# A transformer layer's feed-forward in two phases, all up products first, and the down-projection by seven products of sums

## The chip, the cores and the metric

The kernel runs on one core of a Trainium2 chip. The core has a matrix engine (TensorE, PE in the profile), three engines for elementwise work (VectorE, DVE; ScalarE, ACT; GpSimd, POOL) and a queue engine (SyncE, SP) that issues most transfers between the chip's large memory (DRAM) and the on-chip memory (SBUF). Products are accumulated in PSUM, in banks of 128 x 512 float32. Each engine works through its own instructions in order; engines wait for each other by semaphores. The metric is the device time of one execution in microseconds (us).

## The reference

One layer over 2048 rows of 1024: a retention branch and an attention branch, an output projection, and a feed-forward with a squared ReLU. The change touches the feed-forward, the last lines here:

```python
def _sqrelu_mlp(h, w1, w2):
    return jnp.square(jax.nn.relu(h @ w1)) @ w2
...
    x = x + g1 * (jnp.concatenate([ret, att], axis=-1) @ w_out)
    h2 = _modulate(_rmsnorm(x, norm2_g), sh2, sc2)
    x = x + g2 * _sqrelu_mlp(h2, w_ff1, w_ff2)
...
    return _rmsnorm(x, final_norm_g)
```

`w_ff1` is 1024 x 4096 and `w_ff2` 4096 x 1024. `g2` is one row of 1024 factors, the gate.

## The kernel before

Every float32 factor of a product is written as a sum of two float16 parts, a high one and a low one. The high part is a rounding copy on ScalarE (L70), the low part a subtraction on VectorE or GpSimd (L71). A product is then three TensorE products: high x high, high x low, low x high.

The 2048 rows are 16 tiles of 128, in two halves of 8 (`halves`). The hidden width is 16 blocks of 256 (`FB`, `NB`), and the loop over `b` runs 32 times: all blocks for the first half, then all for the second. One pass has two parts:

- The up part (`up_part`, L1522 to L1524) multiplies a block of `w_ff1` with the half's activations. It treats both as 2 x 2 block matrices and forms the result from seven products of sums instead of eight products (Winograd's form of Strassen's method). The sums of the activations are made once per half (`h_pair`, by GpSimd and ScalarE) and kept as seven 1 MB tiles `hf`; those of the first half go through DRAM. The sums of w1 are made for each pass by GpSimd (`sum_w1`, L1451) and split by ScalarE and VectorE (`form_w1`, L1460 and L1461). Each of the seven products is 12 matmuls into one bank. `up_out` adds the banks up on VectorE (L1545), applies the ReLU on ScalarE (L1533), squares on GpSimd (L1534) and splits the result into `uhi` and `ulo`.
- The down part (`down`, L1582 to L1584) multiplies the block's 256 hidden columns with 256 rows of `w_ff2`, tile by tile and 512 columns at a time, in the plain way: 16 times 6 matmuls. VectorE adds each bank into one of eight accumulators (L1585). Before that GpSimd multiplies the block of `w_ff2` with the gate (L1506), and ScalarE and VectorE split it (L70, L71 on `ws`).

So one pass has 7 x 12 = 84 up matmuls and 96 down matmuls of 128 x 128 by 128 x 512.

The accumulators start as the tiles' residual rows `x1_d` and stay in SBUF for a half. When the first half ends, each is normalised and stored (`ending`, L1600) and loaded anew for the second half. The second half's activation sums are made during the first half (`pairs`), and the first pass's up products are partly issued during attention (`prelude`). Work that is due at no fixed place, such as the last tile's transposes (L1306) or the endings, goes through the list `rest`, of which a few steps are issued after each product. In this stage the order of instructions on every engine is that in which the Python code issues them; only the stage of input projections at the kernel's start is ordered by a scheduler.

## Time and profile before

| | us |
|---|---|
| median of 3 runs | 2948.83 |
| lowest, highest run | 2946.54, 2952.58 |
| span of the profiled execution | 2938.2 |
| TensorE busy within the span | 2770.0 |
| first up matmul, last down matmul start | 1644.4, 2927.3 |

The span is counted from the first to the last instruction of the profiled execution, the only time that the page gives for it; the runs' times hold some work around it as well. In the profile a row of a group gives the line of the code, engine, operation, the tiles written and read, their shapes and the count; then the busy time in us and the mean of one instruction in ns; then the engine's idle time just before these instructions, and what ended it. A row of a timeline gives start and duration in us, and in brackets the idle time before. A row of windows gives a stretch, its length, and for each engine the busy time in it and the number of instructions.

### The profile page before, as it was taken

Reading aid. Unit: us, or ns where it says so; the run is one execution under the profiler, and the core shown is the slowest. Engines: PE = TensorE matmul, PEld = TensorE weight load, DVE = VectorE, ACT = ScalarE, POOL = GpSimd, SP = SyncE. Lnnn points to the kernel's source line nnn. Section 1 sums busy time; section 2 is a strip of 40 time slices with the busy share of each in tenths; the row PEclk is TensorE's granted clock in tenths of the full one; section 3 lists DMA queues with packets and bytes.
Section 4 is the critical chain, followed back from the end, with each engine's and each line's share of the span. In section 5 each row is a group of like instructions: output and inputs, shape, how many; then the busy total and the mean of one; then the engine's idle time right before and its main releaser. Section 6 shows DMA issues by size and latency. Waiting matters only on the chain. (4 is left out here: it accounts for less than half of the span.)

```text
span 2938.2 us, 45295 instructions
## 1 busy us (share of the span) xinstructions
PE 2770.0 (94%) x17140; PEld 1644.8 (56%) x17140; DVE 2181.9 (74%) x3330; ACT 1389.6 (47%) x2279; POOL 1546.1 (53%) x1275
## 2 busy tenths in 40 slices
PE   7998898998889999999999899999999999999998
PEld 3787677775556666555666444444444344444443
DVE  5889847647887777777876577778777777777776
ACT  2333333325777777787777433333332333333323
POOL 2436426425776668787656656664443444444332
PEclk9999999999999999999999999999999999999999
DMA  8988843526412123332211723331114411111111
GB/s 299 336 291 284 275 154 102 159 69 203 135 43 84 50 63 121 89 102 89 72 64 51 276 90 101 104 105 58 53 51 154 169 64 48 51 51 54 58 44 58
DMA packets 265161, 346.95 MB, mean 118 GB/s; under 512 B 106215, under 2 KB 163815, under 8 KB 263150
## 3 DMA queue, kind: packets, MB, share of 16 engines
q1 hardware_dynamic: 254662, 336.57, 34.6%
q10 hardware_dynamic: 10280, 7.48, 0.9%
q8 instruction: 135, 2.21, 0.3%
q14 instruction: 84, 0.69, 0.1%
HBM read 272.52 MB, written 71.46 MB: 117 GB/s over the span
## 5 line engine op out<-in xcount | busy, mean ns | idle before, releaser
L178 DVE TENSOR_REDUCE nm<-mp 128x1 f32<-128x512 f32 (+1 forms) x576 | 391.1, 685 | 169.0 <-PE mp L165 140.8
L219 POOL TENSOR_TENSOR plo<-p,phi 128x1024 f16<-128x1024 f32 x160 | 352.7, 2205 | 173.4 <-ACT phi L212 131.7
L208 ACT ACTIVATE p<-st 128x512 f32<-128x512 f32 x576 | 338.5, 597 | 188.4 <-PE st L203 116.7
L1582 PE MATMUL pd<-w2hi,uhi 128*128 128x512 f16 x1024 | 388.0, 379 | 11.7 <-DVE acc L1585 10.8
L1583 PE MATMUL pd<-w2lo,uhi 128*128 128x512 f16 x1024 | 388.0, 379 | 0.8 <-DVE w2lo L71 0.8
L1584 PE MATMUL pd<-w2hi,ulo 128*128 128x512 f16 x1024 | 388.1, 379 | 0.0
L1585 DVE SCALAR_TENSOR_TENSOR acc<-pd,sc,acc 128x512 f32<-128x512 f32 x512 | 366.5, 739 | 5.6 <-PE pd L1584 5.6
L1522 PE MATMUL pu<-hf,w1f 128*128 128x512 f16 x896 | 340.3, 380 | 2.4 <-DVE q L1545 2.0
L1524 PE MATMUL pu<-hf,w1f 128*128 128x512 f16 x896 | 340.3, 380 | 0.0
L1523 PE MATMUL pu<-hf,w1f 128*128 128x512 f16 x896 | 340.1, 380 | 0.0
L824 PE MATMUL pso<-whi,hi_l 128*128 128x512 f32 (+1 forms) x768 | 294.1, 386 | 11.5 <-ACT xs L524 6.7
L212 ACT ACTIVATE phi<-p 128x1024 f16<-128x1024 f32 x288 | 304.0, 1055 | 0.0
L826 PE MATMUL pso<-whi,lo_l 128*128 128x512 f32 (+1 forms) x768 | 292.1, 381 | 4.2 <-DVE lo_l L67 4.2
L825 PE MATMUL pso<-wlo,hi_l 128*128 128x512 f32 (+1 forms) x768 | 291.6, 380 | 1.2 <-DVE wlo L67 1.1
L235 PE MATMUL o<-wv,plo 128*128 128x65 f16 x2304 | 235.2, 193 | 25.4 <-POOL plo L219 16.7
L221 DVE TENSOR_TENSOR plo<-p,phi 128x512 f16<-128x512 f32 x256 | 242.7, 949 | 18.9 <-ACT phi L212 16.0
L236 PE MATMUL o<-wv,phi 128*128 128x129 f16 x2304 | 243.0, 220 | 0.0
L235 PEld LDWEIGHTS <-plo 128*128 128x128 f16 x2304 | 206.2, 98 | 59.9 <-POOL plo L219 25.7
L202 PE MATMUL st<-qr,ks 128*128 128x512 f16 x576 | 219.3, 381 | 15.4 <-ACT p L208 15.3
L1534 POOL TENSOR_TENSOR r<-r 128x512 f32<-128x512 f32 x64 | 66.4, 1041 | 294.9 <-ACT r L1533 294.9
L203 PE MATMUL st<-qr,ks 128*128 128x512 f16 x576 | 219.3, 381 | 0.1
L236 PEld LDWEIGHTS <-phi 128*128 128x128 f16 x2304 | 205.4, 97 | 19.9 <-issue 0.3
(324 smaller groups left out, 5734.8 us busy)
## 6 DMA issues: line engine op xcount, KB each, us to landing
wm<-in_w_ff SPq DMA_DIRECT2D x64, 512.0 KB, 5.5
w1r<-in_w_ff SPq DMA_DIRECT2D x64, 512.0 KB, 4.5
ws<-in_w_ff SPq DMA_DIRECT2D x124, 256.0 KB, 3.3
wst<-in_w_in SPq DMA_DIRECT2D x60, 512.0 KB, 5.2
wst<-in_w_mod SPq DMA_DIRECT2D x32, 512.0 KB, 6.0
hf<-hp SPq DMA_DIRECT2D x56, 256.0 KB, 3.1
hf<-hf SPq DMA_DIRECT2D x14, 1024.0 KB, 6.2
orv<-rv SPq DMA_DIRECT2D x35, 256.0 KB, 4.0
```

Source lines behind the costliest of these rows:

```text
L178: nc.vector.tensor_reduce(dst, src, axis=AX.X, op=ALU.max, negate=True)
L208: nc.scalar.activation(self.p[kt // 2][:, kt % 2], self.s.pop(kt), AF.Exp, scale=HD**-0.5)
L219: nc.gpsimd.tensor_tensor(lo, p, hi, op=ALU.subtract)
L235: mm(o[:, : HD + 1], lo[:, i, c], v[:, : HD + 1], start=False, stop=False)
L236: mm(o, hi[:, i, c], v[:, :VW], start=False, stop=last)
L1522: mm(pu[i], whi, hi, start=k == 0, stop=False)
L1523: mm(pu[i], whi, lo, start=False, stop=False)
L1524: mm(pu[i], wlo, hi, start=False, stop=k == 3)
L1582: mm(ps, uh, wh, start=f == 0, stop=False)
L1583: mm(ps, uh, wl, start=False, stop=False)
L1584: mm(ps, ul, wh, start=False, stop=f == NF - 1)
L1585: nc.vector.scalar_tensor_tensor(acc[:, c], ps, sc2, acc[:, c], op0=ALU.mult, op1=ALU.add)
```

## The change

The feed-forward is taken apart into two phases.

Phase one (`up_jobs`) makes all up products. Its passes are called items: blocks 0 to 5 for the first half alone, then blocks 6 to 15 for both halves with one set of w1 forms, then blocks 0 to 5 for the second half alone. While the first items run, the second half's activation sums are made, now straight into SBUF (`form` for half 1, its low parts by turns on GpSimd and VectorE). The squared results are not split but stored to DRAM as float32 (`store_u`). Beside the products `w2_steps` makes the seven forms of each block of `w_ff2` once, split, without the gate, and stores them to DRAM (`wf_d`).

Phase two (`down_jobs`) makes the down-projection. The 16 blocks form four rounds of four (`PLACE`). In each round the seven forms of four blocks stand in SBUF, seven tiles of 1 MB, in the slots that held the activation sums. A round goes through eight pairs of tiles (`PAIRS`). For a pair, four pieces of u are loaded two pairs ahead; GpSimd makes their four sums and ScalarE and VectorE split seven forms one pair ahead (`prepare`); TensorE makes seven products of 12 matmuls (`down`); VectorE adds them up (`down_out`); GpSimd multiplies each of the four 128 x 512 results with the gate and adds it to the tile's rows (`gate`), which are loaded from `x1_d` and stored there again in rounds 0 to 2 (`write`). In round 3 they are normalised and go to the output (`ending`). PSUM has six banks for both phases. The gate and the scale factors are folded together differently in `scales`.

The diff, cut to its core:

```diff
-    hf_d = [scratch(f"hf{i}", 7, [P, 2, 4, 512], F16) for i in range(2)]
+    hf_d = scratch("hf", 7, [P, 2, 4, 512], F16)
+    u_d = [scratch(f"u{i}", 2, [4, P, 4, 4, P]) for i in range(4)]
+    wf_d = [scratch(f"wf{i}", 7, [P, 4, 2, 512], F16) for i in range(4)]
...
         def form(i, w):
+            if hf == 1:
+                f = hs[1, i][:, :, :, j * P : (j + 1) * P]
+                split16(f[:, 0], f[:, 1], x[w], nc.gpsimd if i % 2 else nc.vector)
+                return
...
+    AHEAD = 6
+    ITEMS = [(b, (0,)) for b in range(AHEAD)] + [(b, (0, 1)) for b in range(AHEAD, NB)]
+    ITEMS += [(b, (1,)) for b in range(AHEAD)]
+    PLACE = {b % NB: ((b - AHEAD) // 4, (b - AHEAD) % 4) for b in range(AHEAD, AHEAD + NB)}
...
+        ff["w"] = Ring((pool(early_ff, "fw"), "w", 7))
+        ff["r"] = Ring((pool(early_ff, "fr"), "r", 6))
+        ff["ps"] = Ring((pool(early_ff, "fp1", space=PSUM), "p", 4))
...
+        ff["w"].extend(pool(late_ff, "fw2", side="right"), "w", 3)
+        ff["r"].extend(pool(late_ff, "fr2", side="right"), "r", 5)
+        ff["ps"].extend(pool(late_ff, "fp2", space=PSUM), "p", 2)
...
-    def down(b, m, n, acc):
...
-        nc.vector.scalar_tensor_tensor(acc[:, c], ps, sc2, acc[:, c], op0=ALU.mult, op1=ALU.add)
...
+    def store_u():
+        _, b, hf, blk, r = stores.pop(0)
+        rd, slot = PLACE[b]
+        dst = u_d[rd][hf][:, :, blk, slot].rearrange("q p t -> p q t")
+        nc.sync.dma_start(dst, r.rearrange("p (q t) -> p q t", q=4))
...
+    def w2_steps(b):
+        x = {}
+        rd, slot = PLACE[b]
+        def fetch(f):
+            w = xp.tile([P, D], F32, name="w2r", tag="hb", bufs=2)
+            nc.sync.dma_start(w, a["w_ff2"][0, b * FB + f * P : b * FB + (f + 1) * P, :])
+            x[f"b{f + 1}1"], x[f"b{f + 1}2"] = w[:, :512], w[:, 512:]
+        def add(to, p, q, at=None):
+            x[to] = x[at] if at else xp.tile([P, 512], F32, name="w2s", tag="hu", bufs=3)
+            nc.gpsimd.tensor_tensor(x[to], x[p], x[q], op=ALU.subtract)
+        def form(i, w):
+            f = xp.tile([P, 2, 512], F16, name="w2f", tag="hp", bufs=2)
+            nc.scalar.activation(f[:, 0], x[w], AF.Copy, scale=scw)
+            nc.vector.scalar_tensor_tensor(f[:, 1], x[w], scw, f[:, 0], op0=ALU.mult, op1=ALU.subtract)
+            x["made"] = i, f
+        def store():
+            if "made" in x:
+                i, f = x.pop("made")
+                nc.sync.dma_start(wf_d[rd][i][:, slot], f)
+        steps = [(add, "t1", "b12", "b11"), (form, 0, "b11"), (add, "t2", "b22", "t1")]
+        steps += [(form, 5, "t1"), (add, "t3", "b22", "b12", "b12"), (form, 2, "t2"), (add, "t4", "b21", "t2", "t1")]
+        steps += [(form, 1, "b21"), (form, 3, "t3"), (form, 6, "b22"), (form, 4, "t4")]
+        def step(fn, *at):
+            store()
+            fn(*at)
+        return [lambda f=f: fetch(f) for f in range(2)] + [lambda at=at: step(*at) for at in steps] + [store]
...
+    def up_jobs():
+        pairs = [step for j in range(4) for step in h_pair(1, j)]
+        later = [step for b in PLACE for step in w2_steps(b)]
+        owed = 0.0
+        for n, (b, halves_) in enumerate(ITEMS):
+            both = len(halves_) == 2
+            if 1 in halves_:
+                rest_steps(len(rest))
+                while pairs:
+                    pairs.pop(0)()
+            last0 = max(m for m, (_, h) in enumerate(ITEMS) if 0 in h)
+            for i in range(4 if n == 0 else 0, 7):
+                for hf in halves_:
+                    for k in range(4):
+                        up_part(n, i, hf, k)
+                    ff["job"] += 1
+                    while stores and stores[0][0] < ff["job"] - 1:
+                        store_u()
+                    if hf == halves_[-1]:
+                        if n > 0 and i < 4:
+                            sum_w1(n + 1, *SUMS1[i])
+                        if n > 0 or i > 3:
+                            form_w1(n + 1, i)
+                        if i == 4:
+                            fetch_w1(n + 2)
+                    up_out(n, i, hf)
+                    if rest:
+                        rest_steps(2)
+                    elif pairs:
+                        pairs.pop(0)()
+                        if pairs and i % 2:
+                            pairs.pop(0)()
+                    elif later and n > AHEAD - 1:
+                        owed += 1.5
+                        while later and owed >= 1:
+                            owed -= 1
+                            later.pop(0)()
+                    if n == last0 + 1:
+                        fetch_w2(0, i)
+                    if n == len(ITEMS) - 1:
+                        prepare(0, i - 1)
+            if n == len(ITEMS) - 2:
+                assert not later, len(later)
+                for blk in RAW:
+                    fetch_u(0, blk)
+                fetch_y(0)
+        while later:
+            later.pop(0)()
+        while stores:
+            store_u()
+        prepare(0, 6)
...
+    def fetch_w2(rd, i):
+        w = w2[rd, i] = ff["h"][rd % 2].tile([P, 4, 2, 512], F16, name="w2", tag="hf")
+        nc.sync.dma_start(w, wf_d[rd][i])
+    def fetch_u(p, blk):
+        if p < len(PAIRS):
+            rd, hf, q = PAIRS[p]
+            if "raw" not in rings:
+                rings["raw"] = Ring((xp, "w1s", 4), (xp, "hu", 3))
+                rings["sum"] = Ring((xp, "hp", 2), (xp, "u", 2))
+                rings["y"] = Ring((xp, "xr", 3), (xp, "hb", 2))
+            w = raw2[p, NAMES[blk]] = rings["raw"].tile([P, 4, P], F32, "ur")
+            nc.sync.dma_start(w, u_d[rd][hf][q, :, blk])
+    def fetch_y(p):
+        if p < len(PAIRS):
+            for g, t in enumerate(tiles_of(p)):
+                y = ys[p, g] = rings["y"].tile([P, D], F32, "y")
+                nc.sync.dma_start(y, x1_d[t])
+    def sum_u(p, to, x, y, op, at=None):
+        s = raw2[p, to] = raw2[p, at] if at else rings["sum"].tile([P, 4, P], F32, "us")
+        nc.gpsimd.tensor_tensor(s, raw2[p, x], raw2[p, y], op=op)
+    def prepare(p, i):
+        if p >= len(PAIRS) or i < 0:
+            return
+        if i == 0:
+            sum_u(p, "s1", "a21", "a22", ALU.add)
+            sum_u(p, "s2", "s1", "a11", ALU.subtract)
+        if i == 1:
+            sum_u(p, "s3", "a11", "a21", ALU.subtract, "a21")
+        if i == 3:
+            sum_u(p, "s4", "a12", "s2", ALU.subtract, "s2")
+        u = uf[p, i] = ff["w"].tile([P, 2, 4, P], F16, "uf")
+        split16(u[:, 0], u[:, 1], raw2[p, FORMS2[i]])
+    def down(p, i):
+        rd = PAIRS[p][0]
+        ps = pu[i] = ff["ps"].tile([P, 512], F32, "pd")
+        u, w = uf.pop((p, i)), w2[rd, i]
+        for b in range(4):
+            mm(ps, u[:, 0, b], w[:, b, 0], start=b == 0, stop=False)
+            mm(ps, u[:, 0, b], w[:, b, 1], start=False, stop=False)
+            mm(ps, u[:, 1, b], w[:, b, 0], start=False, stop=b == 3)
+    def down_out(p, i):
+        ps = pu.pop(i)
+        def add(x, to=None):
+            to = to if to is not None else ff["r"].tile([P, 512], F32, "d")
+            nc.vector.tensor_tensor(to, ps, xs_[x], op=ALU.add)
+            return to
+        if i == 0:
+            xs_["x"] = ff["r"].tile([P, 512], F32, "d")
+            nc.scalar.activation(xs_["x"], ps, AF.Copy)
+        elif i == 1:
+            gates.append((p, 0, 0, add("x")))
+        elif i == 2:
+            xs_["u2"] = add("x")
+        elif i == 3:
+            xs_["u3"] = add("u2")
+        elif i == 4:
+            gates.append((p, 1, 0, add("u3")))
+        elif i == 5:
+            gates.append((p, 1, 1, add("u3", xs_["u3"])))
+            add("u2", xs_["u2"])
+        elif i == 6:
+            gates.append((p, 0, 1, add("u2", xs_["u2"])))
+    def gate(fast=False):
+        p, g, n, c = gates.pop(0)
+        s = slice(n * 512, (n + 1) * 512)
+        y = ys[p, g][:, s]
+        eng = nc.vector if fast else nc.gpsimd
+        eng.tensor_tensor(c, c, ff["g2"][:, s], op=ALU.mult)
+        eng.tensor_tensor(y, y, c, op=ALU.add)
+        if PAIRS[p][0] < 3:
+            if (g, n) in ((1, 1), (0, 1)):
+                written.append((p, g))
+            return
+        if n == 0:
+            sums[p, g] = ff["sm"].tile([P, 2], F32, name="ss", tag=f"ss{g}")
+        junk = ff["sm"].tile([P, 512], BF16, name="junk", tag="junk", bufs=1)
+        nc.scalar.activation(junk, y, AF.Square, accum_out=sums[p, g][:, n : n + 1])
+        if n == 1:
+            ending(p, g)
+    def write():
+        p, g = written.pop(0)
+        nc.sync.dma_start(x1_d[tiles_of(p)[g]], ys.pop((p, g)))
+    def ending(p, g):
+        ss, y, t = sums.pop((p, g)), ys.pop((p, g)), tiles_of(p)[g]
+        rest.append((lambda: nc.vector.tensor_tensor(ss[:, :1], ss[:, :1], ss[:, 1:], op=ALU.add),))
+        steps = []
+        r = rsqrt_chain(ss[:, :1], 1, 1.0 / D, "e", steps)
+        rest.extend((step,) for step in steps)
+        def whole(c):
+            nc.vector.scalar_tensor_tensor(y[:, c], y[:, c], r, ff["fg"][:, c], op0=ALU.mult, op1=ALU.mult)
+        def store(c):
+            nc.sync.dma_start(out[0, t * P : (t + 1) * P, c], y[:, c])
+        if p == len(PAIRS) - 1:
+            for i in range(2):
+                c = slice(i * 512, (i + 1) * 512)
+                rest.extend([(whole, c), (store, c)])
+        else:
+            c = slice(0, D)
+            rest.extend([(whole, c), (lambda: None,), (store, c)])
+    def down_jobs():
+        for i in range(7):
+            fetch_w2(1, i)
+        for blk in RAW:
+            fetch_u(1, blk)
+        for p, (rd, hf, q) in enumerate(PAIRS):
+            final = p == len(PAIRS) - 1
+            for i in range(7):
+                down(p, i)
+                prepare(p + 1, i)
+                if i in (2, 3, 4, 5):
+                    fetch_u(p + 2, RAW[i - 2])
+                rest_steps(3)
+                if i == 5:
+                    fetch_y(p + 1)
+                while gates and not final:
+                    gate()
+                down_out(p, i)
+                if final:
+                    while gates:
+                        gate(i > 4)
+                if written and i in (1, 2):
+                    write()
+                if (hf, q) == (1, 3) and rd in (0, 1):
+                    fetch_w2(rd + 2, i)
+        while gates:
+            gate(True)
+        rest_steps(len(rest))
```

328 lines of the change are left out of this document (92 added, 236 removed).

## The prediction

> **What bounds the kernel now.** I read the page first: its head, then the chain that ended last.
>
> ```profile
> span 2938.2 us, 45295 instructions
> PE 2770.0 (94%) x17140; PEld 1644.8 (56%) x17140; DVE 2181.9 (74%) x3330; ACT 1389.6 (47%) x2279; POOL 1546.1 (53%) x1275
> PE 32%; DVE 2%; ACT 1%; issue 1%; POOL 0%; DMA 0%; SPq 0%; DVEq 0%; POOLq 0%; ACTq 0%
> ```
>
> TensorE fills the span and the chain, whose six largest lines are the feed-forward's products. Shares over the span say nothing of one stage, so next the windows view (us; busy time and count on PE, PEld, DVE, ACT, POOL; granted clock; DMA share; GB/s).
>
> ```profile
> 1630.00:1650.00 20.00, 19.16 (x134) 10.40 (x132) 11.94 (x22) 10.35 (x21) 11.83 (x13) 1.00 1.03 414
> 1680.00:1705.00 25.00, 20.07 (x90) 8.66 (x89) 23.01 (x29) 8.57 (x15) 15.40 (x12) 1.00 0.83 307
> 1770.00:1790.00 20.00, 18.96 (x88) 8.45 (x87) 15.63 (x21) 6.82 (x11) 13.90 (x10) 1.00 0.68 197
> 2280.00:2335.00 55.00, 47.85 (x210) 20.77 (x209) 44.90 (x54) 21.87 (x37) 23.77 (x21) 0.97 0.48 168
> 2306.00:2312.00 6.00, 4.94 (x16) 1.90 (x16) 5.07 (x7) 1.96 (x3) 2.22 (x2) 0.72 0.55 199
> 2340.00:2900.00 560.00, 560.00 (x2596) 253.79 (x2594) 412.50 (x546) 181.44 (x288) 226.09 (x172) 1.00 0.16 51
> 2598.99:2637.84 38.85, 38.85 (x182) 17.64 (x181) 28.87 (x39) 12.61 (x20) 15.82 (x14) 1.00 0.17 54
> ```
>
> From 2340 to 2900 TensorE never rests, while VectorE has a quarter free and GpSimd more than half. The last row is one block of 256 hidden columns, from one start of its GpSimd sums to the next: 84 up and 96 down products in 38.85 us, 0.2158 us each. (The window touches 182 of them at its edges.) TensorE rests only in the first block (4.9 us), at 1780 (1.0) and at the turn between the halves (7.2).
>
> The page says nothing of what GpSimd and VectorE do to each other; the timelines of the two engines at the block's start do.
>
> ```profile
> 2597.30 1.73 POOL L1506 TENSOR_TENSOR ws<-ws,g2b 128x512 f32<-128x512 f32 x1
> 2598.99 1.27 POOL L1451 TENSOR_TENSOR w1s<-w1r 128x512 f32<-128x512 f32 x1
> 2600.34 1.60 POOL L1451 TENSOR_TENSOR w1s<-w1s,w1r 128x512 f32<-128x512 f32 x1
> 2637.84 1.27 POOL L1451 TENSOR_TENSOR w1s<-w1r 128x512 f32<-128x512 f32 x1
> ...
> 2599.14 1.67 DVE L1461 SCALAR_TENSOR_TENSOR w1f<-w1r,sc,w1f 128x512 f16<-128x512 f32 x1
> 2600.74 0.74 DVE L1585 SCALAR_TENSOR_TENSOR acc<-pd,sc,acc 128x512 f32<-128x512 f32 x1
> 2603.73 0.68 DVE L71 TENSOR_TENSOR w2lo<-ws,w2hi 128x512 f16<-128x512 f32 x1
> 2604.99 0.74 DVE L1461 SCALAR_TENSOR_TENSOR w1f<-w1s,sc,w1f 128x512 f16<-128x512 f32 x1
> ```
>
> L1461 takes 0.74 us alone and 1.67 us when it starts beside the sum at 2598.99; it ends 0.55 us behind it. The next sum starts meanwhile and takes 1.60 us instead of 1.27. L1585, which reads PSUM, takes 0.74 us beside a busy GpSimd. So GpSimd and a VectorE instruction with two SBUF inputs take turns, and a turn costs GpSimd up to 1.73 - 1.27 = 0.46 us; PSUM readers cost it nothing.
>
> **A, products removed.** The up-projection keeps its 2688. The down-projection goes from 3072 to 32 pairs of tiles x 7 x 12 = 2688. 384 x 0.2158 = **-82.9 us**, if TensorE stays the bound.
>
> **B, stalls that lose their cause.** No down product follows the first block and no accumulators are swapped at the turn: -4.9 - 1.0 - 7.2 = **-13.1**. Against that, the last tile's transposes move one product (12 matmuls) ahead, to a place where TensorE already waits:
>
> ```profile
> 1678.56 0.66 PE L1306 MATMUL bank<-ident,xr 128*128 128x128 f32 x4 [3.88 <-POOL xr L1301]
> ```
>
> 12 x 0.2158 = **+2.6**; between 0 and 2.6, as the store that L1301 waits for meets fewer loads.
>
> **C, hand-over between the phases.** SP issues, in this order: the last stores of u, the seven 1 MB forms of w2 for round 1 (they wait for TensorE's last use of the slots), then u for pair 1. ScalarE's split of that u stands ahead of its copy of pair 0's first product, so with six PSUM banks TensorE stops after six products, 6 x 2.59 = 15.5 us.
>
> ```profile
> L1545 DVE TENSOR_TENSOR q<-pu,q 128x512 f32<-128x512 f32 x64 | 43.3, 677 | 0.0
> L1533 ACT ACTIVATE r<-r,scu 128x512 f32<-128x512 f32 x64 | 45.8, 722 | 152.2 <-DVE r L1545 152.1
> L1534 POOL TENSOR_TENSOR r<-r 128x512 f32<-128x512 f32 x64 | 66.4, 1041 | 294.9 <-ACT r L1533 294.9
> L70 ACT ACTIVATE uhi<-r 128x512 f16<-128x512 f32 x64 | 39.4, 616 | 3.7 <-POOL r L1534 3.7
> L1550 ACT ACTIVATE v<-pu 128x512 f32<-128x512 f32 x32 | 18.5, 577 | 12.3 <-PE pu L1524 12.3
> hf<-hf SPq DMA_DIRECT2D x14, 1024.0 KB, 6.2
> hb<-h SPq DMA_DIRECT2D x16, 512.0 KB, 5.7
> ```
>
> The last store can go one addition, one relu and one square after the last up product: 0.7 + 0.7 + 1.0 = 2.4 us. Then 7.34 MB at the 414 GB/s of the first window take 17.7 us, and three pieces of u (0.79 MB) 1.9. One 1 MB load lands after 6.2 us where its bytes would need 2.5, so 3.7 of latency are added. Split and copy take 1.2. Pair 0's first bank is free at 2.4 + 17.7 + 1.9 + 3.7 + 1.2 = 26.9, and TensorE has stood 26.9 - 15.5 = 11.4. A stopped TensorE also loses clock: in the row 2306:2312 the grant is 0.72, that is 3.4 of 6.0 us at half rate, 1.7 us lost. Together **+13.1**; between 4 (if the u of pair 1 gets past the loads in front of it by more than half their time) and 20 (if the seven loads run at 300 GB/s, as around 1680 to 1705).
>
> [...]
>
> **D, GpSimd in phase two.** A pair gives TensorE 84 x 0.2158 = 18.13 us. GpSimd gets 12 operations of two SBUF inputs: four sums of u, and gate and addition for four pieces. (Before, the gate went onto w2.) Free, they take 12 x 1.27 = 15.2. VectorE makes seven low parts per pair, each with two SBUF inputs, and a GpSimd that hardly pauses meets all of them: 15.2 + 7 x 0.46 = **18.4**, just above TensorE's 18.13. VectorE's other seven instructions read PSUM and take no turn. VectorE itself has 7 x about 1.2 (between the 0.68 and 1.67 above) + 7 x 0.68 = 13.2, ScalarE 7 x 0.62 + 0.58 = 4.9; both stay below TensorE. Round 3 adds two roots and two whole-row scalings:
>
> ```profile
> L1506 POOL TENSOR_TENSOR ws<-ws,g2b 128x512 f32<-128x512 f32 x120 | 187.5, 1584 | 13.6 <-DMA ws<-in_w_ff 13.6
> L1009 POOL TENSOR_SCALAR cv_e<-ss 128x2 f32<-128x2 f32 x6 | 1.2, 194 | 30.8 <-ACT junk L1594 30.8
> L1010 POOL TENSOR_TENSOR cy_e<-cv_e,half 128x1 f32<-128x1 f32 x1 | 0.5, 549 | 0.1
> 2929.86 1.29 DVE L1600 SCALAR_TENSOR_TENSOR acc<-acc,cy_e,fgb 128x1024 f32<-128x1024 f32 x1 [1.02 <-POOL cy_e L1010]
> ```
>
> The roots take 2 x (0.19 + 0.55) = 1.5. L71's 0.68 us hold GpSimd for 0.46, so 0.22 of an instruction hold nothing; L1600's 1.29 then hold 1.07, two of them 2.1. Round 3 asks 18.4 + 3.6 = 22.0 per pair. GpSimd's lag grows by 0.27 x 24 pairs = 6.5, then by 3.9 x 7 = 27; the last pair, without sums or low parts, wins back some 5. Six banks and u's lead of a pair let TensorE run ahead for a while, but what lag is not worked off is paid at the end: **+28**. At a mean price x for the twelve operations the term is 31 x (12x - 18.13) + 7 x 3.6 - 5 = 372x - 542. Its ends are 0 (at 1.27 round 3 needs 18.8 at most, which the banks cover) and 102 (every operation at 1.73). L1506's mean of 1.584 would give 47; I take 18.4 / 12 = 1.53, because there are only seven turns for twelve operations. A root also waits for ScalarE's square and VectorE's sum of it, with the next gates behind it: up to 1 us each, taken as 0 where the next pair's sums stand in between, 7 to 14 if not.
>
> **E, first items of phase one.** In items 1 to 5 (one half, 18.13 us) GpSimd has four squares at L1534's 1.04 (4.2), four sums of w1 (5.1), ten of the thirteen steps of a second-half tile pair (10/13 of four sums and three low parts, 6.9) and some ten turns (4.5):
>
> ```profile
> L71 POOL TENSOR_TENSOR hp<-hb,hp 128x512 f16<-128x512 f32 x32 | 42.4, 1327 | 19.2 <-ACT hp L70 14.0 <-issue 5.2
> ```
>
> That is 20.7 us, a lag of 13 over five items, and each pair's loads (5.7 us for hb) hold up the sums behind them. Forms are made a whole item ahead and six banks hide about 13 us; items 6 to 15 (36.3 us, some 29 of GpSimd's and 30 of VectorE's work, w2's forms included) win it back. **+4**; between 0 and 22 (four loads not hidden). Without those roomy items w2's forms would cost their GpSimd time.
>
> **F, the rest.** At the end gate and addition stand behind the last product on VectorE, 2 x 0.68 = **+1.4**. Phase two moves 3.1 MB per pair, 174 GB/s; round changes add 7.3 MB and 7 us of backlog, hidden by u's two pairs of lead. The scheduler reorders a few projections: 0, plus or minus 3.
>
> **Sum.** -82.9 - 13.1 + 2.6 + 13.1 + 28 + 4 + 1.4 = -46.9: the span of 2938.2 becomes 2891.3. The runs' median of 2948.83 lies 10.6 above the profiled span; with that kept, the time is **2902**.
>
> **Rivals.** (1) GpSimd never binds: turns fall into its pauses, D = 0, **2874**. For it: 226 of 560 us busy before. Against: 15.2 of 18.13 leave few pauses. (2) The first items starve: E at 22, **2920**; six banks speak against it. (3) Slower: in phase two every GpSimd operation pays a turn, at 1.73 as in the row at 2597.30; D = 102, **2976**. Terms other than D leave 74.9 us of gain, so the point is 372x - 542 = 75, an average of 1.66 us per operation: only 0.13 above what I take. For it: L1506's mean is already 1.584. Against: seven turns in twelve operations.
>
> **Chances.** Forecast 0.47 (alone 2882 to 2925), rival 1 0.20, rival 2 0.13, rival 3 0.15, others 0.05. The range 2866 to 2950 holds the first three and leaves out rival 3 and some tails. 0.2% (6 us) is what a measurement here can tell: faster 0.78, same 0.05, slower 0.17.
>
> **What would show it.** A: 5376 feed-forward products, 0.216 us apart. C: one TensorE gap of about 12 us at the first down products, ended by ScalarE, behind a load of u. D: GpSimd some 18 us busy per pair, its group means near 1.5; TensorE gapless in rounds 0 to 2 and waiting in round 3. E: no gap before item 6. Wrong if gaps appear in rounds 0 to 2, if the gate and addition average over 1.66, or if round 3 runs at 18.1 us per pair.

## The result, and the profile after

The changed kernel takes 3031.53 us in the median of 4 runs (3028.91 to 3033.76); the kernel before, run beside it, 2947.68 us (2945.55 to 2952.58). The ratio is 1.0284, with a 95% interval of 1.0269 to 1.0299: 84 us slower. The forecast was 2902 us, with a range of 2866 to 2950.

The page of the changed kernel, its head and the chain that ended last:

```profile
span 3027.1 us, 45947 instructions
PE 2731.4 (90%) x16756; PEld 1614.5 (53%) x16756; DVE 2045.8 (68%) x3086; ACT 1409.7 (47%) x2349; POOL 1933.3 (64%) x1549
POOL 1%; issue 0%; DVE 0%; ACT 0%; POOLq 0%; DVEq 0%
```

TensorE has less work than before (2731.4 us against 2770.0), and the span has grown by 88.9. No engine is full on average, and the shares of the chain do not say where TensorE stood still. The windows do, when they are cut at the first products of the stages (columns as in the prediction; the last two cuts lie within 0.5 us of theirs). First the kernel before, from a gap that both traces show in the last tile of attention: the first item's 84 up products and what stands among them, then the rest.

```profile
1639.19:1681.65 42.46, 36.69 (x177) 17.29 (x177) 19.82 (x29) 16.39 (x32) 23.75 (x23) 1.00 0.81 301
1681.65:2938.20 1256.55, 1231.17 (x5681) 556.02 (x5679) 936.67 (x1216) 426.02 (x685) 565.88 (x433) 1.00 0.24 79
```

Then the changed kernel: from the same gap to item 1; items 1 and 2; items 3 to 5; items 6 to 16; item 17; pair 0 of phase two; pairs 1 to 24 (rounds 0 to 2); pairs 25 to 30 (round 3).

```profile
1639.32:1694.10 54.78, 42.89 (x181) 19.95 (x181) 20.49 (x28) 15.89 (x31) 18.73 (x18) 0.84 0.52 192
1694.10:1730.36 36.26, 36.26 (x171) 16.43 (x169) 19.16 (x23) 16.03 (x27) 29.82 (x23) 1.00 0.43 138
1730.36:1806.13 75.77, 59.84 (x254) 25.59 (x253) 44.01 (x52) 29.56 (x49) 46.14 (x36) 0.93 0.41 125
1806.13:2249.30 443.17, 398.80 (x1764) 174.41 (x1764) 280.82 (x333) 191.29 (x294) 260.00 (x195) 0.97 0.55 174
2249.30:2282.00 32.70, 20.21 (x85) 8.53 (x85) 18.76 (x21) 13.15 (x21) 19.06 (x14) 0.89 0.94 353
2358.16:2400.09 41.93, 20.77 (x85) 8.83 (x84) 14.00 (x17) 9.64 (x17) 12.56 (x10) 0.73 0.70 260
2400.09:2835.22 435.13, 435.13 (x2015) 197.19 (x2014) 280.90 (x336) 107.48 (x189) 425.73 (x289) 1.00 0.62 207
2835.22:2988.20 152.98, 123.89 (x508) 52.31 (x507) 80.74 (x107) 42.05 (x96) 103.87 (x95) 0.91 0.38 118
```

The way to read them is to set a stage's length beside 0.2158 us for each of its products. Items 1 and 2 (168 products, 36.25 us) and pairs 1 to 24 (18.13 us each) run at TensorE's own pace. Items 6 to 16 have 1764 products, 380.7 us, and take 443.17. No other engine is busy for even two thirds of that stretch. The clock is part of it: the mean grant of 0.97 is worth some 13 us of the 443.17. (The products' busy time, 398.80 us, is 18 above 380.7; the part that the clock does not explain is, as an estimate, the end of the matmul before each rest, since a matmul shows 0.386 us in the group view below but starts 0.2158 us behind the one before.) So a stretch in which everyone has time loses 62 us; the group view of items 6 to 16 shows who waits for whom.

```profile
L1503 PE MATMUL pu<-hf,w1f 128*128 128x512 f16 x588 | 226.8, 386 | 43.1 <-DVE r L1515 37.7 <-ACT hf L70 4.7
L1515 DVE TENSOR_TENSOR r<-pu,r 128x512 f32<-128x512 f32 x147 | 97.3, 679 | 0.0
L1519 ACT ACTIVATE r<-r,scu 128x512 f32<-128x512 f32 x84 | 60.1, 721 | 151.5 <-DVE r L1515 151.5
L1520 POOL TENSOR_TENSOR r<-r 128x512 f32<-128x512 f32 x84 | 91.4, 1091 | 151.4 <-ACT r L1519 146.8 <-DMA wf<-w2f 2.6 <-DMA w1r<-in_w_ff 2.0
```

TensorE waits for VectorE's additions to free a bank. The additions themselves wait for nothing that this view names (0.0), and ScalarE's relu stands idle 1.8 us before each of 84 for them. The timelines of the two engines at the turn from item 11 to item 12 show what is late (start, duration, instruction, in brackets the idle time before it):

```profile
2056.63 0.68 DVE L1515 TENSOR_TENSOR r<-pu,r 128x512 f32<-128x512 f32 x1
2058.71 0.75 DVE L1564 SCALAR_TENSOR_TENSOR w2f<-w2s,scw,w2f 128x512 f16<-128x512 f32 x1 [1.40 <-ACT w2f L1563]
2059.38 1.53 DVE L1488 SCALAR_TENSOR_TENSOR w1f<-w1r,sc,w1f 128x512 f16<-128x512 f32 x1
2060.83 0.68 DVE L1515 TENSOR_TENSOR r<-pu,r 128x512 f32<-128x512 f32 x1
2062.90 1.02 DVE L1564 SCALAR_TENSOR_TENSOR w2f<-w2s,scw,w2f 128x512 f16<-128x512 f32 x1 [1.40 <-ACT w2f L1563]
2063.85 1.28 DVE L1515 TENSOR_TENSOR r<-pu,r 128x512 f32<-128x512 f32 x2
...
2057.34 0.72 ACT L1519 ACTIVATE r<-r,scu 128x512 f32<-128x512 f32 x1 [1.57 <-DVE r L1515]
2057.97 0.71 ACT L1563 ACTIVATE w2f<-w2s,scw 128x512 f16<-128x512 f32 x1
2061.54 0.72 ACT L1519 ACTIVATE r<-r,scu 128x512 f32<-128x512 f32 x1 [2.25 <-DVE r L1515]
2062.17 0.70 ACT L1563 ACTIVATE w2f<-w2s,scw 128x512 f16<-128x512 f32 x1
```

VectorE adds (to 2057.31), ScalarE starts the relu at 2057.34 and, behind it, the high part of a form of w2; VectorE stands 1.40 us for that high part, makes the low part, makes a low part of w1, and only then, at 2060.83, the next addition. One turn of this loop takes 4.20 us, the next 3.02. One job of TensorE, a product of 12 matmuls, takes 2.59; over the whole stretch a job took 443.17 / 147 = 3.01. Every engine is idle for part of each turn, and the six banks run full.

Phase two has two more places. At the hand-over, from the timelines of GpSimd, SP and ScalarE:

```profile
2369.61 1.04 POOL L1520 TENSOR_TENSOR r<-r 128x512 f32<-128x512 f32 x1 [1.98 <-ACT r L1519]
...
2361.61 9.42 SPq L1544 DMA_DIRECT2D u<-r  x4
2371.12 3.70 SPq L1670 DMA_DIRECT2D w<-wf  x7
2374.88 23.47 SPq L1680 DMA_DIRECT2D ur<-u  x8
...
2393.85 0.63 ACT L70 ACTIVATE uf<-ur 128x512 f16<-128x512 f32 x1 [23.29 <-DMA ur<-u]
2394.39 0.58 ACT L1733 ACTIVATE d<-pd 128x512 f32<-128x512 f32 x1
```

The windows from TensorE's last product before its rest on:

```profile
2373.49:2376.90 3.41, 0.38 (x2) 0.10 (x1) 0.00 (x0) 0.00 (x0) 0.00 (x0) 1.00 1.01 399
2376.90:2395.02 18.12, 0.00 (x0) 0.00 (x0) 0.50 (x1) 1.17 (x3) 1.74 (x2) 0.51 1.02 413
2395.02:2400.90 5.88, 5.88 (x14) 2.08 (x14) 5.57 (x8) 2.77 (x5) 5.80 (x4) 0.50 0.30 83
```

ScalarE stands 23.29 us for the first piece of u of pair 1, with the copy of pair 0's first product right behind it; TensorE's rest ends 0.05 us after that copy. And in round 3, from the timelines of GpSimd, ScalarE and VectorE in pair 28:

```profile
2927.91 1.26 POOL L1755 TENSOR_TENSOR d<-d,g2b 128x512 f32<-128x512 f32 x1
2929.25 1.26 POOL L1756 TENSOR_TENSOR y<-y,d 128x512 f32<-128x512 f32 x1
2935.55 0.19 POOL L1009 TENSOR_SCALAR cv_e<-ss 128x1 f32<-128x1 f32 x1 [3.81 <-DVE ss L1776]
...
2930.55 0.63 ACT L1764 ACTIVATE junk<-y 128x512 bf16<-128x512 f32 x1 [5.62 <-POOL y L1756]
2931.18 0.58 ACT L1733 ACTIVATE d<-pd 128x512 f32<-128x512 f32 x1
2931.65 0.62 ACT L70 ACTIVATE uf<-ur 128x512 f16<-128x512 f32 x1
...
2932.30 0.69 DVE L71 TENSOR_TENSOR uf<-ur,uf 128x512 f16<-128x512 f32 x1 [5.27 <-ACT uf L70]
2934.11 0.68 DVE L1728 TENSOR_TENSOR d<-pd,d 128x512 f32<-128x512 f32 x1
```

It is the same figure with other engines: ScalarE stands 5.62 us for a gated half, to square it; the copy and the high part stand behind the square; VectorE stands 5.27 us for the high part; its addition stands behind the low part; and GpSimd then stands for VectorE. GpSimd is busy for 103.87 of 152.98 us there.

### The profile page after: what moved, and what is told of

Its sections match the earlier page's. It is cut to its first block, busy times and chain, and to the rows that moved or that the text cites. A ratio compares the mean times of both kernels' runs of the same rounds, so it can differ in the third digit from the quotient of the medians.

```text
span 3027.1 us, 45947 instructions
## 1 busy us (share of the span) xinstructions
PE 2731.4 (90%) x16756; PEld 1614.5 (53%) x16756; DVE 2045.8 (68%) x3086; ACT 1409.7 (47%) x2349; POOL 1933.3 (64%) x1549
## 5 line engine op out<-in xcount | busy, mean ns | idle before, releaser
L1503 PE MATMUL pu<-hf,w1f 128*128 128x512 f16 x896 | 347.9, 388 | 73.3 <-DVE r L1515 68.0
L1715 PE MATMUL pd<-w,uf 128*128 128x512 f16 x896 | 345.9, 386 | 51.8 <-ACT d L1733 44.5
L1504 PE MATMUL pu<-hf,w1f 128*128 128x512 f16 x896 | 347.6, 388 | 1.3 <-POOL hf L71 1.1
L1505 PE MATMUL pu<-hf,w1f 128*128 128x512 f16 x896 | 347.5, 388 | 0.0
L1716 PE MATMUL pd<-w,uf 128*128 128x512 f16 x896 | 345.7, 386 | 0.0
L1717 PE MATMUL pd<-w,uf 128*128 128x512 f16 x896 | 345.5, 386 | 0.0
L824 PE MATMUL pso<-whi,hi_l 128*128 128x512 f32 (+1 forms) x768 | 294.7, 386 | 10.5 <-ACT xs L526 4.7
L1520 POOL TENSOR_TENSOR r<-r 128x512 f32<-128x512 f32 x128 | 137.6, 1076 | 248.2 <-ACT r L1519 243.6
L223 DVE TENSOR_TENSOR plo<-p,phi 128x512 f16<-128x512 f32 x256 | 240.1, 939 | 18.4 <-ACT phi L214 15.8
L71 DVE TENSOR_TENSOR uf<-ur,uf 128x512 f16<-128x512 f32 x128 | 143.3, 1130 | 160.7 <-ACT uf L70 160.6
L167 PE MATMUL mp<-ks,qr 128*128 128x512 f16 x512 | 196.1, 383 | 23.5 <-DVE nm L180 23.4
```

Source lines behind the costliest of these rows:

```text
L824: mm(ps[:, :width], hi[:, k], wh, start=k == 0, stop=False)
L1503: mm(pu[hf, i], whi, hi, start=k == 0, stop=False)
L1504: mm(pu[hf, i], whi, lo, start=False, stop=False)
L1505: mm(pu[hf, i], wlo, hi, start=False, stop=k == 3)
L1715: mm(ps, u[:, 0, b], w[:, b, 0], start=b == 0, stop=False)
L1716: mm(ps, u[:, 0, b], w[:, b, 1], start=False, stop=False)
```

## The experiments

Profiled executions differ by up to 9 us before they reach the changed code, so single spans are compared from the gap in attention's last tile on. Each row below is one execution; in stages that an edit does not touch, rows differ by up to about 3 us (pairs 0 to 2: 21.0 to 24.3). The table gives, for every kernel, the time from that gap to item 1, then for each stage its time beyond 0.2158 us a product, then the time from the last product's start to the end, and the whole time from the gap to the end (us):

| kernel | to item 1 | items 3-6 | 7-16 | 17 | 18-21 | pairs 0-2 | 25-31 | tail | gap to end |
|---|---|---|---|---|---|---|---|---|---|
| changed kernel | 54.8 | 32.8 | 51.1 | 14.6 | 3.6 | 24.3 | 45.4 | 19.3 | 1387.8 |
| u first | 54.9 | 32.7 | 53.3 | 15.1 | 3.6 | 9.1 | 49.4 | 19.3 | 1379.9 |
| square 1 later | 53.1 | 32.8 | 51.5 | 15.0 | 3.7 | 21.0 | 26.1 | 19.4 | 1364.4 |
| relu 1 later | 53.1 | 17.7 | 7.4 | 12.2 | 3.7 | 19.1 | 45.5 | 19.3 | 1319.7 |
| one round of w2 | 52.6 | 32.5 | 11.5 | 0.0 | 0.0 | 18.2 | 46.6 | 19.2 | 1322.4 |
| relu, sums, loads | 54.6 | 13.0 | 2.0 | 4.0 | 4.1 | 18.8 | 46.2 | 19.3 | 1303.9 |
| prelude, two gates | 51.3 | 33.1 | 52.6 | 15.3 | 3.7 | 23.1 | 19.5 | 16.9 | 1357.4 |
| all | 47.4 | 14.9 | 0.1 | 0.7 | 4.1 | 0.0 | 15.4 | 17.0 | 1241.4 |
| all, one gate | 48.2 | 12.2 | 3.8 | 4.6 | 0.1 | 0.0 | 19.0 | 18.5 | 1248.3 |
| all, square 3 later | 48.5 | 15.0 | 0.1 | 3.3 | 4.1 | 0.0 | 11.0 | 19.1 | 1243.0 |
| square 3 later alone | 54.5 | 32.7 | 52.6 | 15.5 | 3.6 | 23.4 | 16.2 | 19.0 | 1359.5 |
| ScalarE squares u | 48.3 | 11.5 | 0.1 | 2.5 | 4.1 | 0.0 | 11.1 | 18.8 | 1238.3 |

The kernel before takes 42.5 to its first item's end and 1299.0 from the gap to the end. Pairs 3 to 24 lose nothing in any kernel (0.6 in one).

**The relu one job later.** The one edit that separates the loop from the work in phase one: nothing is added or removed. `relu` issues the three lines that are taken out here, so GpSimd's square and the store of u move with the relu.

```diff
         def done(r, f, tg):
-            nc.scalar.activation(r, r, AF.Relu, scale=scu)
-            nc.gpsimd.tensor_tensor(r, r, r, op=ALU.mult)
-            stores.append((ff["job"], ITEMS[n][0], hf, 2 * tg + f, r))
+            relus.append((n, r, hf, 2 * tg + f))
...
                     while stores and stores[0][0] < ff["job"] - 1:
                         store_u()
+                    while relus:
+                        relu()
```

> Only phase one is touched: each relu and its square on GpSimd are issued one job later, so ScalarE no longer waits within a job for VectorE's add of that job. Theory of the loop (add on VectorE, relu on ScalarE, a high part behind the relu, the low part on VectorE, the next add behind that, 3.0 to 4.3 us against a job's 2.59): items 6 to 17, which lose 77 us, lose under 40, and the span falls by 35 to 60 us. Rival: what holds these items is the waits for loads of w2 and for w1's sums on GpSimd; then items 6 to 17 lose 60 or more and the span falls by less than 15 us.

Items 6 to 16 took 392.68 us instead of 443.17, items 6 to 17 lost 24.2 instead of 77.1, and from the gap to the end the kernel gained 68.1 us, more than the 60 expected at most, because items 3 to 5 lost 13.2 instead of 21.4 and pairs 0 to 2 lost 19.1 instead of 24.3. Items 6 to 16 and item 17 in the windows view of this kernel:

```profile
1798.22:2190.90 392.68, 382.82 (x1764) 172.33 (x1764) 279.41 (x333) 191.19 (x294) 265.49 (x195) 1.00 0.61 197
2190.90:2221.18 30.28, 19.20 (x84) 8.17 (x84) 16.08 (x21) 13.14 (x21) 18.20 (x14) 0.96 0.95 367
```

VectorE, ScalarE and GpSimd are as busy as before (280.82, 191.29 and 260.00 us); only the order of waits changed. The loop is shown; with the rests gone the grant is 1.00 and the products' busy time 382.82. Item 17 (second row) still lost 12.2.

**Only one round of w2's forms.** This kernel makes the forms of four blocks of `w_ff2` and multiplies with them in all four rounds; the other twelve blocks are left out.

```diff
-        later = [step for b in PLACE for step in w2_steps(b)]
+        later = [step for b in list(PLACE)[:4] for step in w2_steps(b)]
...
-        nc.sync.dma_start(w, wf_d[rd][i])
+        nc.sync.dma_start(w, wf_d[0][i])
```

> Leaves out the forms of w2 for rounds 1 to 3: only the first four blocks' forms are made (56 steps of 224, in items 6 to 9), and all four rounds read them, so the products and the loads of phase two are as before. It prices the w2 steps. Theory of the loop: without them items 10 to 17 lose under 1 us each, and the span falls by about 40 us (what items 10 to 17 lose now: 9.2, 2.2, 6.2, 4.3, 7.0, 4.4, 4.0 and 14.6, sum 52, less what item 17 loses by other loads). Rival: the stores and loads of u, or w1's sums, hold these items; then they still lose 3 us or more each.

Items 10 to 21 lost nothing at all, item 17 included. In the timelines above w2's high and low parts stand in the loop; without them the relu, the high parts of w1 and the additions keep up. The edit takes away w2's loads, differences and stores as well, so it prices w2's steps together; that the order of the relu matters is shown by the run before it. From the gap to the end 65.4 us were gained, more than the 40 expected, because item 17 gave back all of its 14.6 us, most of which the expectation had put down to other loads, and items 18 to 20 and the hand-over lost less too. The rival falls: u's stores and w1's sums were all still there.

**The sums a job earlier, the first 1 MB loads two items later**, on top of the later relu.

```diff
-                        if n > 0 and i < 4:
-                            sum_w1(n + 1, *SUMS1[i])
+                        if n > 0 and i < 3:
+                            for one in SUMS1[:2] if i == 0 else SUMS1[i + 1 : i + 2]:
+                                sum_w1(n + 1, *one)
...
-                    if n == last0 + 1:
+                    if n == last0 + 3:
                         fetch_w2(0, i)
```

> On top of the kernel with the later relu (span 2961.1), w1's sums on GpSimd are issued a job before the form that reads them, and the seven 1 MB loads of w2's forms for round 0 start in item 18 instead of item 16. Theory: ScalarE's waits of 3.75 to 4.2 us for a sum that stands behind the tile pairs' work cause what items 3 to 6 still lose (2.2, 5.9, 5.1, 4.6, sum 17.7): they fall below 6 in all; and the loss of item 17 (12.2, ScalarE waiting 6.2 us for the store of a form of w2 that lands behind the 1 MB loads) falls below 2. Span 2961 - 12 - 10, near 2939. Rival for items 3 to 6: GpSimd is simply full with sums and low parts, so the order is of no use and they still lose 12 or more. Rival for item 17: the steps of w2 themselves; then it still loses 8 or more.

Item 17 fell from 12.2 to 4.0, not under 2. Two edits stand behind that, but the row names the loads: in the kernel with the later relu, ScalarE's timeline shows there a high part behind the landing of a form's store.

```profile
2218.36 0.72 ACT L1568 ACTIVATE w2f<-w2r,scw 128x512 f16<-128x512 f32 x1 [6.20 <-DMA wf<-w2f]
```

Items 3 to 6 fell only from 17.7 to 13.0: here the rival's number came true, the sums' place is not what holds them.

**u ahead of the 1 MB loads.**

```diff
-        for i in range(7):
-            fetch_w2(1, i)
         for blk in RAW:
             fetch_u(1, blk)
+        for i in range(7):
+            fetch_w2(1, i)
```

> Pair 0 lasts 41.93 us in the changed kernel (18.13 without a rest), and its one gap of 21.5 us ends when u's pieces of pair 1, issued behind seven 1 MB loads of w2's forms, have landed. Theory of order: the pieces are late because they stand behind 7 MB in the queue; issued ahead of them, pair 0 takes 18 to 24 us and the span falls by 16 to 24 us; the seven loads then land in pair 0, one round before they are read. Rival, bandwidth: the DMA engines are full at the hand-over whatever the order, the stall moves to pair 1 or 2, and pairs 0 to 2 together stay over 72 us; span within 6 us of 3027.

The windows row of pair 0:

```profile
2365.74:2391.86 26.12, 21.12 (x85) 8.61 (x84) 14.31 (x17) 10.05 (x17) 11.60 (x9) 0.88 0.62 214
```

Pair 0 took 26.12 us instead of 41.93, and pairs 0 to 2 lost 9.1 instead of 24.3, with 63.5 us together where the rival said over 72: order, not bandwidth. It is 26 rather than under 24 by one wait of TensorE for ScalarE's copy, 4.5 us, and the lower clock (a mean grant of 0.88 in the row). Of the 15.2 us, 7.9 reached the end: round 3 lost 4.0 more, and items 7 to 16 lost 2.2 more, which lie ahead of the edit and so are a difference between executions. The span fell by 3.0 us only, as the rival had it, but this execution's gap came 4.9 us later.

**The square later, one job and three jobs.** GpSimd's instructions are untouched in both. The diff is that of three jobs; one job later, each job issues what the job before it left.

```diff
+        squares.append((ff["job"], p, g, n, y))
...
+    def square():
+        _, p, g, n, y = squares.pop(0)
         junk = ff["sm"].tile([P, 512], BF16, name="junk", tag="junk", bufs=1)
         nc.scalar.activation(junk, y, AF.Square, accum_out=sums[p, g][:, n : n + 1])
...
                 prepare(p + 1, i)
+                ff["job"] += 1
+                while squares and squares[0][0] <= ff["job"] - 3:
+                    square()
```

> Only round 3 is touched: ScalarE's square of a gated half is issued one job later, behind the high part of the next job, with GpSimd's work unchanged. Theory of the loop (a wait in ScalarE's program order: GpSimd's gate and add, then the square, then the high part behind it, then VectorE's low part and its next add, then GpSimd again): pairs 25 to 30, 25.1 us on average, fall to 18.1 to 20, and the span by 30 to 45 us. Rival, the prediction's throughput theory (GpSimd has 22.0 us of work for each of these pairs): no change, pairs 25 to 30 stay at 22 or more and the span falls by less than 10 us.

> The changed kernel with nothing but the square three jobs later: all gates on GpSimd. It tells how much of round 3 is GpSimd's own work. If GpSimd is the bound as the prediction had it, pairs 27 to 30 stay at its work and its waits, 20.0 + 3.1 = 23.1 us, as with the square one job later. If the loop was still holding it, they fall to 20 to 21, GpSimd's busy time with few waits. At 18.1 to 19 neither is right.

Pairs 27 to 30 in the windows view, first of the changed kernel:

```profile
2884.86:2987.99 103.13, 82.15 (x337) 34.60 (x336) 54.58 (x72) 28.04 (x64) 69.54 (x64) 0.91 0.38 121
```

With the square one job later:

```profile
2878.55:2970.88 92.33, 78.07 (x337) 33.52 (x337) 57.66 (x72) 28.42 (x64) 80.24 (x65) 0.96 0.43 137
```

And three jobs later:

```profile
2882.29:2967.66 85.37, 74.44 (x337) 32.79 (x336) 75.25 (x73) 28.94 (x64) 82.38 (x65) 1.00 0.44 142
```

25.78, 23.08 and 21.34 us a pair. One job later gave 23.08, the rival's number, while the 23.4 us gained from the gap to the end lie between the two expectations; the whole of round 3 lost 26.1 us instead of 45.4. Three jobs later GpSimd is busy 82.38 of 85.37 us and waits for nothing: now it is full, at 21.34 a pair. So about 29 of the 45.4 us were the loop (45.4 - 16.2). The other 16 stand beside a full GpSimd, whose work the prediction had put at 22.0 us a pair. That work is not a fixed amount: for about the same instructions GpSimd's 69.54 us became 82.38 and VectorE's 54.58 became 75.25. The gated addition (L1756) has a mean of 1.26 us in the first of these rows' stretches and 1.87 with the square three jobs later (2860 to 2975). That this comes from more turns between two engines that now rest less is the author's estimate; no row shows the cause. Whether GpSimd's work alone sets the 21.34 is taken up again below.

**Forms out of the prelude, and two gates of four on VectorE** (with the square one job later).

```diff
-        eng = nc.vector if fast else nc.gpsimd
+        eng = nc.vector if fast or (PAIRS[p][0] == 3 and n == 0) else nc.gpsimd
...
-            on(k0 + 20 + 2 * i, "late", sum_w1, 1, *SUMS1[i])
-            on(k0 + 22 + 3 * i, "late", form_w1, 1, i)
+            on(k0 + 24 + 2 * i, "late", sum_w1, 1, *SUMS1[i])
```

> Two places of the changed kernel. First, the first four forms of w1's second item and its sums go back behind the first item's, as they stood in the kernel before: theory, the 12.5 us that the first item lost against the kernel before came from ScalarE and VectorE held by forms that wait for a load and for TensorE; item 1 then starts near 1682 to 1685 instead of 1694. Rival: it came from the last tiles' own order; start within 2 us of 1694. Second, round 3 with the later square, and the first half of each gate (two of four per pair) on VectorE: the throughput theory of the rest (19.98 us of GpSimd work and 3.1 us of its waits, 23.08 a pair) takes off 2 x (1.40 + 1.95) and half of the waits for VectorE: GpSimd needs about 15.5, VectorE 14.3 + 2.8 = 17.1, and pairs 26 to 30 fall from 23.08 to 18.1 to 18.6. Rival, VectorE becomes the bound in the order of its own chain: pairs stay above 20.

The way to item 1 took 51.3 us instead of 54.8, where kernels without this edit show 52.6 to 54.9: what the first item loses is not settled by it. Pairs 28 to 30 took 21.84 us each, not under 18.6, with VectorE busy 86% of the time and GpSimd 65%: the rival's number, though neither engine is full.

**All of it together**, with u's second load moved into the last item of phase one and the 1 MB loads spread over round 0.

```diff
+                        if i == 4:
+                            for blk in RAW:
+                                fetch_u(1, blk)
...
-        for i in range(7):
-            fetch_w2(1, i)
-        for blk in RAW:
-            fetch_u(1, blk)
...
+                if p < 7 and i == 6:
+                    fetch_w2(1, p)
```

> All of it together, with u's pieces for pair 1 loaded in the last item of phase one and the 1 MB loads for round 1 spread over round 0, one a pair. By the theories: the changed kernel's losses against TensorE's own pace are about 12 (first item) + 100 (items 3 to 20) + 24 (hand-over) + 45 (round 3) = 181 us; the edits leave about 0 + 12 + 5 + 3, so the span falls from 3027 to near 2866, about 72 us under the kernel before. If the losses trade places (an engine that is freed in one stage starves the next), the span stays above 2900.

The span is 2889.8. From the gap on the kernel takes 146.4 us less than the changed kernel and 57.6 less than the kernel before. It missed 2866: 9 us are this execution's later gap, and items 3 to 6 and round 3 kept more than expected. At the hand-over nothing was lost.

**Two refinements**: one gate of four on VectorE, w1's first sum and its loads still earlier. The diff shows the first.

```diff
-        eng = nc.vector if fast or (PAIRS[p][0] == 3 and n == 0) else nc.gpsimd
+        eng = nc.vector if fast or (PAIRS[p][0] == 3 and (g, n) == (1, 0)) else nc.gpsimd
```

> The kernel with all edits (span 2889.8), with two refinements. In round 3 one gate of four per pair stays on VectorE instead of two: with two, VectorE is busy 18.9 of 21.8 us and GpSimd 14.2, with none GpSimd is busy 20.0 of 23.1 and VectorE 14.3; with one the two are level at about 16.6 and 17.1, and pairs 27 to 30 fall from 21.84 to 18.1 to 19.5. In phase one the first of w1's sums is made in the last job of the item before, and w1's loads start a job earlier: items 3 to 6, which still lose 14.9, lose under 6. Span near 2890 - 9 - 10 = 2871. Rival for items 3 to 6: the sum's start was not what is late (GpSimd, with sums, squares, differences and low parts, is full for a job of 2.59 us); they still lose 10 or more. Rival for round 3: it is the turns between the two engines, not their work; pairs stay at 21 or more.

Pairs 28 to 30 took 22.46 us and items 3 to 6 lost 12.2: both rivals' numbers, and in round 3 a loss (21.84 before). Against the kernel before the ratio was 0.9822 (0.9805 to 0.9838).

**The square three jobs later, in the kernel with one gate moved** (w1's sums as in the kernel with all edits).

> As the kernel with one gate of four on VectorE in round 3 (with w1's sums as they were in the kernel with all edits), but each square is issued three jobs after its gate instead of one. There no engine is full (of 21.8 us, VectorE 17.0 and GpSimd 16.4) and pairs 28 to 30 still take 22.46. Theory of the loop: ScalarE still reaches the square before GpSimd has made its input and waits up to 6 us, with the high parts of the next pair behind it; three jobs later it finds it made, and pairs 28 to 30 fall to 18.1 to 19.0; span near 2890 - 12 = 2878. Rival, the turns and waits between GpSimd and VectorE themselves: pairs stay above 21.

```profile
2764.64:2845.04 80.40, 73.65 (x337) 32.84 (x336) 71.46 (x78) 26.66 (x59) 63.92 (x53) 1.00 0.47 151
```

Pairs 25 to 27 lost nothing, pair 28 took 19.8 us and pairs 29 and 30 21.25: the loop had a share, but in the end the rival's number comes back, with VectorE busy 89% and GpSimd 80% of the stretch. In each of pairs 29 and 30 GpSimd had 17.09 us of work, against 20.6 with the square three jobs later and all gates on it, and still they took 21.25 us beside 21.34. So GpSimd's work, although it filled that kernel, is not shown to be what holds these pairs; VectorE's work there, 18.7 us a pair in this kernel and 18.8 in that one, lies above TensorE's 18.13, too. What sets these last 3 us a pair is open. This kernel runs in 2885.68 us (2879.63 to 2886.95) against 2944.39 for the kernel before, a ratio of 0.9794 (0.978 to 0.9807). It is faster than the kernel before and than the changed kernel.

**u's square on ScalarE in items 0 to 6.**

```diff
-        nc.gpsimd.tensor_tensor(r, r, r, op=ALU.mult)
+        if n <= AHEAD:
+            nc.scalar.activation(r, r, AF.Square)
+        else:
+            nc.gpsimd.tensor_tensor(r, r, r, op=ALU.mult)
```

> The kernel with all edits and the square three jobs later (span 2885.2), with u's square in items 0 to 6 on ScalarE instead of GpSimd. In items 4 and 5, which last 22.8 and 21.7 us, GpSimd is busy 18.5 and 19.6 us, above TensorE's 18.13, and ScalarE 12.1 and 10.6. Theory: what items 3 to 6 still lose (1.6, 4.7, 3.5, 5.2, sum 15.0) is GpSimd's work for the tile pairs, w1's sums and the squares; without four squares of 1.04 us an item it is under 16, and they lose under 5 in all. Rival: an order of waits holds them whatever GpSimd has to do; they still lose 10 or more. Span near 2885 - 11 = 2874.

```profile
1729.22:1789.31 60.09, 55.22 (x253) 24.63 (x252) 40.38 (x50) 38.90 (x64) 39.03 (x27) 1.00 0.52 155
```

GpSimd's work in items 3 to 5 fell from 52.73 of 64.20 us to 39.03 of 60.09, and items 3 to 6 still lost 11.5 instead of 15.0: GpSimd's amount of work is not what holds most of it. What does stays open. The time, 2884.75 us and a ratio of 0.9794 (0.9776 to 0.9812), is that of the kernel without it.

## Why the prediction was wrong, by its steps

The terms of the sum beside what the trace gives, in us:

| term | predicted | measured |
|---|---|---|
| A, products removed | -82.9 | -82.9 |
| B, stalls of before, first item | -10.5 | -20.8 + 12.3 = -8.5 |
| C, hand-over | +13.1 | +24.3 |
| D, GpSimd in phase two | +28 | +45.4 |
| E, phase one | +4 | +102.1 |
| F, end | +1.4 | +8.4 |
| sum | -46.9 | +88.8 |

(B: before, 1245.7 us from the first down product to the last, less 1224.9 for the 5676 products of both kinds in between; and 54.8 - 42.5.) The sum is one of spans. To get from the span to the time, the prediction added 10.6 us, the distance between the median before and one profiled execution; in the changed kernel's four runs the time lies 1.8 us above the same run's span (3028.91 and 3027.1 in the profiled one). The rest of the 10.6 was a difference between executions, and the span grew by 88.9 where the median grew by 84.

**A held**, 5376 products at 0.2158 us. **B held in size by luck**: 20.8 us went where 13.1 were forecast (14.9 of them TensorE's rest, counted over the whole stretch and not in three places of it), and the first item lost 12.3 where 2.6 were forecast; the two misses nearly cancel.

**E is the step that failed.** It said that the lag of the first items is hidden by banks and forms, and that "items 6 to 15 ... win it back", because GpSimd has 29 and VectorE 30 us of work in 36.3. Work was the wrong measure. These ten items lost 5.9 us each on average, with no engine but TensorE above two thirds. What the step left out is the order inside a job: addition, relu, a high part behind the relu, a low part that waits for it, and the next addition behind that, 3.0 to 4.2 us against a job's 2.59. The later relu, with the same work, took 44 of the 51 us of items 7 to 16. The number that should have warned stood in the prediction's own rows: ScalarE's relu (L1533) waited 152.1 us for VectorE in 64 instances, 2.4 us each. Before, that cost nothing, because an up product's output came every 38.85 / 7 = 5.55 us; the change took the down products from between and left 2.59. The prediction counted the stalls that lose their cause and not the waits that lose their cover. In the rows of the loop VectorE keeps to the order of its instructions: it stands 1.40 us before a low part, while the next addition, for which the group view names no wait (0.0), stays behind it.

**C had the mechanism and one term too small.** The gap came where it was forecast and was ended by ScalarE behind a load of u; TensorE stopped 15.5 us behind the last up product, as worked out, and the loads took 22.7 us (2371.12 to 2393.85; forecast 17.7 + 1.9 + 3.7). The term that failed is the last store, put at 2.4 us after the last up product: it went at 2371.03, 13.1 us after 2357.95, because the same loop held the last relus and squares: VectorE's last additions start at 2359.03, 2362.05, 2365.07 and 2368.09, each behind a low part of pair 0's forms that waits for ScalarE, and the last square starts at 2369.61. The clock cost more, too: after the stop the grant was 0.50 for the 5.88 us behind the restart, 2.9 us lost instead of 1.7. The 1.7 was taken from a rest of 2.04 us in the kernel before, where the grant was 0.50 from 2308.5 to 2311.5, behind the restart at 2307.06. At the hand-over it fell 3.0 to 3.6 us into the rest: it was 1.00 from the last matmul's end at 2373.87 to 2376.90 (first of the three window rows), and the second row's 0.51 leaves at most half a microsecond more.

**D was right for rounds 0 to 2 and close on the work in round 3, wrong about what binds there.** Forecast was 18.4 us of GpSimd a pair; it was 425.73 / 24 = 17.7, and TensorE did not rest. Rival 3 needed a mean of 1.66 us per operation; the mean was 1.47 (425.73 / 289), and the largest groups, gate and addition, stayed below it (group view, pairs 1 to 24):

```profile
L1756 POOL TENSOR_TENSOR y<-y,d 128x512 f32<-128x512 f32 x97 | 157.1, 1619 | 7.6
L1755 POOL TENSOR_TENSOR d<-d,g2b 128x512 f32<-128x512 f32 x96 | 142.0, 1479 | 0.0
```

With the square three jobs later GpSimd is full in round 3 at 21.34 us a pair, beside a forecast of 22.0, and 16 us are lost, not 28: no lag was carried in from rounds 0 to 2 (6.5 of the forecast), and a pair costs 3.2 instead of 3.9, in five pairs instead of seven. That the number is near is partly luck: with 3.5 us of GpSimd's work a pair taken off, the pairs took as long. The other 29 us came from the wait that the change puts on ScalarE: the prediction asked what a root waits for, but not what is queued behind the square.

**F failed as well.** After the last product GpSimd still has gates to make; the chain of the changed kernel shows the last two of its instructions there ending at 3016.52, 8.7 us after the last product's start at 3007.80, where the prediction counted only 1.4 us of VectorE.

```profile
3013.47 1.27 POOL d L1755
3014.82 1.70 POOL y L1756
```

Of the rivals, number 2 had the size of the first items (items 3 to 5 lost 21.4 us; it said 22), which is luck in part, because 8.2 of them went with the later relu and not with a load; and neither it nor the forecast saw the items behind them; the slower rival named an engine that did not bind there. No case had a loop of waits between engines that all have time to spare. Still open are 12 to 15 us of items 3 to 6, the last 3 us of each pair in round 3, about half of what the first item lost (47.4 to 48.5 us in the kernels with all edits, against 42.5), and the end, where nothing was tried.

## What to carry to other kernels

A chain of engines with room to spare was too slow here (items 6 to 16 took 443.17 us, and 392.68 with the relu one job later). For each recurring job, add up one turn of the waits in program order (who stands behind whom on each queue) and set it beside the time that the engine meant to be the bound gives the job. When a change removes work from between two outputs, list the waits that this work covered, in the rows of before, and price them as if it were gone. The cure was cheap here: issue the waiting instruction one to three jobs later, behind the work that does not wait. And put small urgent loads ahead of large ones in a queue (pair 0 took 26.12 us instead of 41.93).

## What the runs showed of the hardware

A tiny VectorE instruction with two SBUF inputs, the sum of two 128 x 1 columns, took 0.15 us while GpSimd stood idle (for 3.81 us before 2909.53) and 1.23 us when it started beside a GpSimd operation of 1.61 us, and then both ended within 0.02 us (rows of both engines' timelines in round 3 of the changed kernel). That is 1.08 us more; the large L1461 in the prediction's rows took 0.93 more beside GpSimd than alone (1.67 and 0.74). In the kernel with the square three jobs later and one gate moved, eight of these sums average 1.22.

```profile
2909.29 0.15 DVE L1776 TENSOR_TENSOR ss<-ss 128x1 f32<-128x1 f32 x1
2925.81 1.23 DVE L1776 TENSOR_TENSOR ss<-ss 128x1 f32<-128x1 f32 x1
2925.41 1.61 POOL L1694 TENSOR_TENSOR us<-us,ur 128x512 f32<-128x512 f32 x1
```

An instruction that reads PSUM showed no such hold: in the kernel before, L1585 takes 0.74 us beside the sum at 2416.75 (L1451), and that sum takes 1.27.
